# An encoder layer on one core: a row of two one-column float32 products at two places, in place of single ones at three

## The chip, the core and the metric

The kernel runs on one core of a Trainium2 chip. The metric is device time in microseconds (us) of one execution; lower is better. The engines that the text names are TensorE (PE, with its weight loads shown apart as PEld), VectorE (DVE), ScalarE (ACT) and SyncE (SP), whose queue issues most of the transfers.

## What is computed

One layer of a bidirectional encoder, for 256 positions of 2048 channels in float32. What matters here are the four large products:

```python
def reference(x, ...):
    h = rmsnorm(x, norm_mix[i])
    p = h @ w_in[i]                                # 2048 -> 4352 columns
    ...                                            # three token mixers give y_a, y_b, y_c
    x = x + jnp.concatenate([y_a, y_b, y_c], axis=-1) @ w_out[i]      # 2048 -> 2048
    h = rmsnorm(x, norm_ffn[i])
    up = dwconv3(h @ ffn_w_up[i], ffn_conv_w[i], ffn_conv_b[i])       # 2048 -> 11264
    gate, val = jnp.split(up, 2, axis=-1)
    x = x + (jax.nn.silu(gate) * val) @ ffn_w_down[i]                 # 5632 -> 2048
    return rmsnorm(x, norm_final)
```

## The kernel before

Activations lie with channels on the 128 partitions and the 256 positions along the free axis. Every large product is made to float32 accuracy from two parts: a weight tile is loaded as float32 (`raw`), ScalarE rounds it to a part `hi` in the type fp32r (line 115), VectorE subtracts to get the rest `lo` (line 116), and the activations are kept in the same two parts side by side. For each block of 128x128 weights TensorE then does two products into one PSUM bank. This **pair** is the unit of all that follows:

```python
            nc.tensor.matmul(ps, hi[:, s], act[:, k, :, :], start=k == 0, stop=False)
            nc.tensor.matmul(ps[:, :L], lo[:, s], act[:, k, 0, :], start=False, stop=k == nk - 1)
```

The first, line 151, streams 512 columns (both parts of the activations), the second, line 152, streams 256. One output tile of 128 channels takes 16 pairs where the input has 2048 channels (input projection, output projection, up-projection), and 44 pairs in the down-projection. The order on TensorE is program order: 16 tiles of the output projection (`yT` is the input), whose first two tiles are interleaved in two halves of 8 pairs each; 88 tiles of the up-projection (`actB`); 12 tiles of the down-projection (`gT`); and then the last 512 output channels in another form (lines 771 to 783).

Between pairs stand a few small float32 products. `sum_cols` (line 176) does two one-column products in a row for a norm's sum of squares, once after the first up-tile; `rms_rows` (line 194) does one product of 256 columns, after the second up-tile; `gate_head` (line 584) does two products of 128 columns in a row, in the input projection. A float32 product shows in the trace as two records. Three more, `settle()` at line 133, are one-column products of a constant tile of ones; nothing reads what they give. One stands after the first 8 pairs of the output projection, one after its first 32 pairs (two tiles), and one after the third up-tile. The scheduler is told to keep them in program order.

Of the kernel before, what the change touches and what calls it, by code (L numbers as in the profile page):

```python
# [54 lines left out]
def encoder_layer(ctx, tc, a):  # L55
    nc = tc.nc
# [11 lines left out]
    def aux():  # L68
        return psa.tile([P, 512], F32, tag="aux", name="aux")
# [20 lines left out]
    ones = const.tile([P, P], F32, name="ones")  # L90
# [39 lines left out]


    def settle():
        tc.keep_in_program_order(nc.tensor.matmul(aux()[:, 0:1], ones, ones[:, 0:1], start=True, stop=True))

    def split(hi, lo, src):
        nc.scalar.copy(hi, src)
# [36 lines left out]
    def sum_cols(acc):  # L173
        pc = aux()
        for h in range(2):
            nc.tensor.matmul(pc[:, h:h + 1], acc[:, h * P:(h + 1) * P], ones[:, 0:1], start=True, stop=True)
        return pc
# [477 lines left out]
    for c in range(2):  # L655
        for m in range(2):
            chunk_products(head[m], w_out(m), yT, c, KT)
            if c == m == 0:
                settle()
    settle()  # L660
    for m in range(KT):
        ps, sb = (head[m], second_half(head[m])) if m < 2 else proj_tile(w_out(m), yT, KT)
        x = xT[:, m, :]
# [23 lines left out]
    for j in range(NFF):  # L687
        o = []
        for part in range(2):
            m = 2 * j + part  # L690
            ps, sb = up[m] if j == 0 else up_tile(m)
            if m == 2:
                settle()
            nc.vector.tensor_add(sb, ps[:, :L], sb)
            s = tmp("ev")
            nc.vector.tensor_mul(s, sb, rbc2)
            o.append(conv3(s, C_FW + m, C_FW + 88 + m, C_FW + 176 + m, C_FB + m, f"o{part + 1}"))
        sg = tmp("gu")
        nc.scalar.activation(sg, o[0], AF.Silu)
        nc.vector.tensor_mul(sg, sg, o[1])  # L700
        split(gT[:, j, 0, :], gT[:, j, 1, :], sg)
# [54 lines left out]
    for h in range(2):  # L756
        acc.append(psm.tile([P, 512], F32, tag="mm", name="mm"))
        for i in range(NL // P):
            nc.tensor.matmul(acc[h][:, i * P:(i + 1) * P], xT[:, MD + i, h * P:(h + 1) * P], ident, start=i == 0,
                             stop=False)  # L760
# [24 lines left out]
    for c in range(NC):  # L785
# [5 lines left out]
        if c == NKEEP:  # L791
            pc = sum_cols(acc3)
# [143 lines left out]
```

## Time and profile before

| | |
|---|---|
| median of 3 runs | 1071.64 us (1071.21 to 1071.91) |
| the profiled execution | 1071.91 us, of it 1070.0 us from the first to the last instruction |
| TensorE busy | 1059.6 us (99%) |
| VectorE, ScalarE busy | 788.9 us (74%), 578.6 us (54%) |
| weight loads (PEld) busy | 923.6 us (86%) |
| moved by DMA | 202.83 MB, 190 GB/s in the mean |
| mean granted TensorE clock | 0.998 |

Busy time of TensorE is modelled and records of neighbouring products overlap, so that 99% does not say at what pace it works. The pace is read from the distance between the starts of two products of the same kind, for instance from one product of line 151 to the next. The trace's times are printed to 0.01 us.

### The profile page before, as it was taken

Reading aid. Unit: us, or ns where it says so; the run is one execution under the profiler, and the core shown is the slowest. Engines: PE = TensorE matmul, PEld = TensorE weight load, DVE = VectorE, ACT = ScalarE, POOL = GpSimd, SP = SyncE. Lnnn points to the kernel's source line nnn. Section 1 sums busy time; section 2 is a strip of 40 time slices with the busy share of each in tenths; the row PEclk is TensorE's granted clock in tenths of the full one; section 3 lists DMA queues with packets and bytes.
Section 4 is the critical chain, followed back from the end, with each engine's and each line's share of the span. In section 5 each row is a group of like instructions: output and inputs, shape, how many; then the busy total and the mean of one; then the engine's idle time right before and its main releaser. Section 6 shows DMA issues by size and latency. Waiting matters only on the chain.

```text
span 1070.0 us, 15760 instructions
## 1 busy us (share of the span) xinstructions
PE 1059.6 (99%) x5974; PEld 923.6 (86%) x5974; DVE 788.9 (74%) x1241; ACT 578.6 (54%) x876; POOL 1.3 (0%) x14
## 2 busy tenths in 40 slices
PE   9999999999999999999999999999999999999997
PEld 9888898888888888888888888888888888888885
DVE  7899998987768778787777777787876454565344
ACT  7766555555556555555555555555555444454332
POOL 0000000000000000000000000000000000000000
PEclk9999999999999999999999999999999999999999
DMA  8776555655666555655566555655565655666452
GB/s 290 244 229 210 161 164 171 232 172 185 196 194 182 186 186 188 182 192 181 193 181 192 181 192 182 190 184 185 189 188 178 190 183 182 225 214 199 142 191 78
DMA packets 61875, 202.83 MB, mean 190 GB/s; under 512 B 6919, under 2 KB 11752, under 8 KB 61672
## 3 DMA queue, kind: packets, MB, share of 16 engines
q1 hardware_dynamic: 61512, 201.45, 59.2%
q8 instruction: 46, 0.75, 0.3%
q10 hardware_dynamic: 288, 0.39, 0.1%
q14 instruction: 29, 0.24, 0.1%
HBM read 199.72 MB, written 2.10 MB: 189 GB/s over the span
## 4 chain that ended last, share of the span: by engine, by line
PE 96%; DVE 1%; DMA 1%; ACT 1%; issue 0%; SPq 0%; DVEq 0%; ACTq 0%
PE mm L151 57%; PE mm L152 29%; PE mm L781 2%; PE mm L783 2%; PE mm L782 2%; PE mm L264 1%; PE mm L263 1%; PE mm L265 1%; DVE lo L116 1%; DMA head<-in_w_v 1%; PE aux L141 0%; PE aux L142 0%; DMA raw<-in_w_in 0%; PE aux L489 0%; PE aux L140 0%
## 5 line engine op out<-in xcount | busy, mean ns | idle before, releaser
L115 ACT CAST hi<-raw 128x1024 fp32r<-128x1024 f32 (+1 forms) x362 | 373.4, 1031 | 443.7 <-PE mm L151 222.8
L116 DVE TENSOR_TENSOR lo<-raw,hi 128x1024 fp32r<-128x1024 f32 (+1 forms) x362 | 434.6, 1201 | 239.6 <-ACT hi L115 239.0
L151 PE MATMUL mm<-actB,hi 128*128 128x512 f32 x1408 | 497.9, 399 | 0.0
L152 PE MATMUL mm<-actB,lo 128*128 128x256 f32 x1408 | 395.3, 281 | 0.0
L151 PEld LDWEIGHTS mm<-actB,hi 128*128 128x128 f32 x1408 | 264.5, 188 | 66.0 <-DVE actB L668 0.3
L152 PEld LDWEIGHTS mm<-actB,lo 128*128 128x128 f32 x1408 | 265.9, 189 | 0.0
L151 PE MATMUL mm<-gT,hi 128*128 128x512 f32 x528 | 186.6, 399 | 0.0
L152 PE MATMUL mm<-gT,lo 128*128 128x256 f32 x528 | 148.3, 281 | 0.0
L151 PE MATMUL mm<-actA,hi 128*128 128x512 f32 x416 | 148.0, 398 | 0.0
L151 PEld LDWEIGHTS mm<-gT,hi 128*128 128x128 f32 x528 | 99.2, 188 | 24.8
L152 PE MATMUL mm<-actA,lo 128*128 128x256 f32 x416 | 116.2, 279 | 0.0
L152 PEld LDWEIGHTS mm<-gT,lo 128*128 128x128 f32 x528 | 99.7, 189 | 0.0
L151 PEld LDWEIGHTS mm<-actA,hi 128*128 128x128 f32 x416 | 78.1, 188 | 16.9
L151 PE MATMUL mm<-yT,hi 128*128 128x512 f32 x256 | 89.3, 395 | 0.0
L152 PEld LDWEIGHTS mm<-actA,lo 128*128 128x128 f32 x416 | 78.5, 189 | 0.1
L152 PE MATMUL mm<-yT,lo 128*128 128x256 f32 x256 | 71.0, 278 | 0.0
L408 ACT ACTIVATE o<-ev,par 128x256 f32<-128x256 f32 x106 | 63.4, 598 | 7.2 <-DVE ev L403 5.7
L151 PEld LDWEIGHTS mm<-yT,hi 128*128 128x128 f32 x256 | 48.0, 188 | 11.1
L410 DVE SCALAR_TENSOR_TENSOR o<-ev,par,o 128x255 f32<-128x255 f32 x106 | 51.2, 483 | 3.3
L159 ACT COPY sb<-mm 128x256 f32<-128x256 f32 x142 | 51.8, 365 | 0.0
L409 DVE SCALAR_TENSOR_TENSOR o<-ev,par,o 128x255 f32<-128x255 f32 x106 | 50.7, 478 | 0.4 <-ACT o L408 0.4
L152 PEld LDWEIGHTS mm<-yT,lo 128*128 128x128 f32 x256 | 48.1, 188 | 0.0
(226 smaller groups left out, 819.2 us busy)
## 6 DMA issues: line engine op xcount, KB each, us to landing
raw<-in_w_up SPq DMA_DIRECT2D x176, 512.0 KB, 3.5
raw<-in_w_down SPq DMA_DIRECT2D x60, 512.0 KB, 3.6
raw<-in_w_in SPq DMA_DIRECT2D x56, 512.0 KB, 3.6
raw<-in_w_out SPq DMA_DIRECT2D x32, 512.0 KB, 3.5
raw<-in_w_last SPq DMA_DIRECT2D x22, 512.0 KB, 3.5
raw<-in_w_v SPq DMA_DIRECT2D x8, 384.0 KB, 4.4
raw<-in_w_down SPq DMA_DIRECT2D x12, 256.0 KB, 2.6
head<-in_w_v SPq DMA_DIRECT2D x7, 384.0 KB, 6.2
```

Source lines behind the costliest of these rows:

```text
L115: nc.scalar.copy(hi[:, s], raw[:, s])
L116: nc.vector.tensor_sub(lo[:, s], raw[:, s], hi[:, s].bitcast(F32))
L151: nc.tensor.matmul(ps, hi[:, s], act[:, k, :, :], start=k == 0, stop=False)
L152: nc.tensor.matmul(ps[:, :L], lo[:, s], act[:, k, 0, :], start=False, stop=k == nk - 1)
L159: nc.scalar.copy(sb, ps[:, L:])
L263: nc.tensor.matmul(o, actA[:, k, 0, t], hi[:, s], start=k == 0, stop=False)
L408: nc.scalar.activation(o, s, AF.Identity, bias=col(b), scale=col(w1))
L409: nc.vector.scalar_tensor_tensor(o[:, 1:], s[:, :L - 1], col(w0), o[:, 1:], op0=ALU.mult, op1=ALU.add)
L410: nc.vector.scalar_tensor_tensor(o[:, :L - 1], s[:, 1:], col(w2), o[:, :L - 1], op0=ALU.mult, op1=ALU.add)
L781: nc.tensor.matmul(acc[h], lh, hi[:, s], start=False, stop=False)
L782: nc.tensor.matmul(acc[h], lh, lo[:, s], start=False, stop=False)
L783: nc.tensor.matmul(acc[h], ll, hi[:, s], start=False, stop=False)
```

## The change

`settle()` now issues two one-column products in a row, into two columns of one PSUM tile, where it issued one. The call after the two first output tiles is gone. So there are two places with two products each, where there were three places with one.

```diff
     def settle():
-        tc.keep_in_program_order(nc.tensor.matmul(aux()[:, 0:1], ones, ones[:, 0:1], start=True, stop=True))
+        pc = aux()
+        for h in range(2):
+            tc.keep_in_program_order(nc.tensor.matmul(pc[:, h:h + 1], ones, ones[:, 0:1], start=True, stop=True))
...
             chunk_products(head[m], w_out(m), yT, c, KT)
             if c == m == 0:
                 settle()
-    settle()
     for m in range(KT):
         ps, sb = (head[m], second_half(head[m])) if m < 2 else proj_tile(w_out(m), yT, KT)
```

On TensorE, at the first place in the output projection, between the first half of tile `mm_2523` and that of `mm_2524`, the order before was:

```order
L152 MATMUL mm_2523<-yT_519,lo_2527 128x256
L151 MATMUL mm_2523<-yT_519,hi_2526 128x512
L152 MATMUL mm_2523<-yT_519,lo_2527 128x256
L133 MATMUL aux_2547<-ones_85 128x1
L151 MATMUL mm_2524<-yT_519,hi_2550 128x512
L152 MATMUL mm_2524<-yT_519,lo_2551 128x256
```

and in the changed kernel, where lines from 133 on have moved down by one or two numbers, it is:

```order
L154 MATMUL mm_2523<-yT_519,lo_2527 128x256
L153 MATMUL mm_2523<-yT_519,hi_2526 128x512
L154 MATMUL mm_2523<-yT_519,lo_2527 128x256
L135 MATMUL aux_2547<-ones_85 128x1 x2
L153 MATMUL mm_2524<-yT_519,hi_2551 128x512
L154 MATMUL mm_2524<-yT_519,lo_2552 128x256
```

One product has become two at the same spot. Also on TensorE, after the third tile of the up-projection (`mm_3529` before, `mm_3528` in the changed kernel), the order before was:

```order
L152 MATMUL mm_3529<-actB_2521,lo_3554 128x256
L151 MATMUL mm_3529<-actB_2521,hi_3553 128x512
L152 MATMUL mm_3529<-actB_2521,lo_3554 128x256
L133 MATMUL aux_3576<-ones_85 128x1
L151 MATMUL mm_3585<-actB_2521,hi_3587 128x512
L152 MATMUL mm_3585<-actB_2521,lo_3588 128x256
```

and it is now:

```order
L154 MATMUL mm_3528<-actB_2521,lo_3553 128x256
L153 MATMUL mm_3528<-actB_2521,hi_3552 128x512
L154 MATMUL mm_3528<-actB_2521,lo_3553 128x256
L135 MATMUL aux_3575<-ones_85 128x1 x2
L153 MATMUL mm_3585<-actB_2521,hi_3587 128x512
L154 MATMUL mm_3585<-actB_2521,lo_3588 128x256
```

Here too only the second product is added. After the first two output tiles, where the second of the three single products stood, pairs now follow on pairs. The orders of VectorE, ScalarE, GpSimd and SyncE are the same as before.

## Rows read from the trace of the kernel before

**Rows 1.** The page: the span, TensorE's share, the chain that ended last.

```profile
span 1070.0 us, 15760 instructions
PE 1059.6 (99%) x5974; PEld 923.6 (86%) x5974; DVE 788.9 (74%) x1241; ACT 578.6 (54%) x876; POOL 1.3 (0%) x14
...
PE 96%; DVE 1%; DMA 1%; ACT 1%; issue 0%; SPq 0%; DVEq 0%; ACTq 0%
```

**Rows 2.** Line 151 after the third settle: count; durations; first and last start.

```profile
L151 PE MATMUL mm<-actB,hi x1360: 395/398/476, 331.6 to 811.8; 128*128 128x512 f32 x195
L151 PE MATMUL mm<-gT,hi x528: 395/398/403, 812.2 to 998.4; 128*128 128x512 f32 x176
```

**Rows 3.** Line 151 between the second settle and the first wait in the up-projection.

```profile
L151 PE MATMUL mm<-yT,hi x224: 392/395/475, 235.9 to 313.3; 128*128 128x512 f32 x112
L151 PE MATMUL mm<-actB,hi x16: 392/394/395, 313.7 to 318.9; 128*128 128x512 f32 x16
```

**Rows 4.** Engines by stretch: length, busy us (records) by engine, granted clock, DMA share, GB/s.

```profile
236.30:319.10 82.80, 82.80 (x479) 72.38 (x478) 59.05 (x91) 46.61 (x77) 0.00 (x0) 1.00 0.64 194
331.90:998.50 666.60, 666.60 (x3775) 578.11 (x3774) 479.86 (x711) 358.23 (x539) 0.00 (x0) 1.00 0.60 189
```

**Rows 5.** TensorE in order of time (start us, us): third settle, and last pair.

```profile
331.32 0.28 PE L152 MATMUL mm<-actB,lo 128*128 128x256 f32 x1
331.44 0.28 PE L133 MATMUL aux<-ones 128*128 128x1 f32 x2
331.58 0.48 PE L151 MATMUL mm<-actB,hi 128*128 128x512 f32 x1
331.89 0.28 PE L152 MATMUL mm<-actB,lo 128*128 128x256 f32 x1
...
332.71 0.40 PE L151 MATMUL mm<-actB,hi 128*128 128x512 f32 x1
...
333.07 0.40 PE L151 MATMUL mm<-actB,hi 128*128 128x512 f32 x1
...
998.39 0.40 PE L151 MATMUL mm<-gT,hi 128*128 128x512 f32 x1
```

**Rows 6.** TensorE in order of time at the first settle.

```profile
227.10 0.28 PE L133 MATMUL aux<-ones 128*128 128x1 f32 x2
...
227.67 0.40 PE L151 MATMUL mm<-yT,hi 128*128 128x512 f32 x1
...
228.03 0.40 PE L151 MATMUL mm<-yT,hi 128*128 128x512 f32 x1
```

**Rows 7.** TensorE in order of time, from 0.9 us after the second settle.

```profile
236.73 0.39 PE L151 MATMUL mm<-yT,hi 128*128 128x512 f32 x1
...
237.07 0.40 PE L151 MATMUL mm<-yT,hi 128*128 128x512 f32 x1
```

**Rows 8.** TensorE at the two float32 products of the fifth `gate_head`.

```profile
197.87 0.28 PE L152 MATMUL mm<-actA,lo 128*128 128x256 f32 x1
197.99 0.60 PE L584 MATMUL aux<-wsT,vtok 128*128 128x128 f32 x4
198.35 0.48 PE L151 MATMUL mm<-actA,hi 128*128 128x512 f32 x1
```

**Rows 9.** Line 151 in the tile after those products, and in the tile after it.

```profile
L151 PE MATMUL mm<-actA,hi x16: 391/391/476, 198.3 to 203.6; 128*128 128x512 f32 x16
...
L151 PE MATMUL mm<-actA,hi x16: 393/398/478, 204.3 to 209.7; 128*128 128x512 f32 x16
```

**Rows 10.** TensorE around `sum_cols`, after the first up-tile.

```profile
318.89 0.40 PE L151 MATMUL mm<-actB,hi 128*128 128x512 f32 x1
...
319.35 0.50 PE L151 MATMUL mm<-actB,hi 128*128 128x512 f32 x1
...
319.81 0.50 PE L176 MATMUL aux<-ones,acc 128*128 128x1 f32 x4
320.17 0.48 PE L151 MATMUL mm<-actB,hi 128*128 128x512 f32 x1
```

## The prediction

> **What bounds the kernel.** The page comes first: TensorE is busy in 99% of the span, the chain that ended last is TensorE in 96%, and nothing waits long [rows 1]. So time can only come from what TensorE does, and the few float32 products that change are too short to matter by themselves. The question is whether the pairs of lines 151 and 152 always take the same time. The view by line, cut into stretches, says no. The granted clock is 1.00, that is 2.4 GHz, in both of the stretches that I compare, and the pairs are of the same shapes in both [rows 4], yet their pace differs:
>
> - After the second settle the pairs start at 236.73, 237.07, ..., 318.89 [rows 7, 10]. By the count these are 237 steps (240 starts of line 151, of which 236.73 is the third) [rows 3]: 82.16 us / 237 = 0.3467 us a pair. The steps alternate between 0.34 and 0.35.
> - After the third settle they start at 332.71, 333.07, ..., 998.39 [rows 5]. From 333.07, the fifth of 1360 + 528 = 1888 starts [rows 2], it is 665.32 us / 1883 = 0.3533 us a pair. One step in three is 0.36.
>
> I call these the fast and the slow pace. Each is kept without a break until something else comes between two pairs: the slow one lasts from 331.58 to 998.39 through 1888 pairs, over a change of the input from `actB` to `gT`, so it is not the operands' place that sets it. VectorE is busy 480 of 667 us there, 72%, as in the fast stretch (59.1 of 82.8, 71%), and the DMA share is lower (0.60 against 0.64) [rows 4]: no supplier holds the slow stretch back. The pace is a state of TensorE, and what stands between the pairs switches it.
>
> **What switches it.** I read TensorE in order of time at each interruption.
>
> - First settle, one product: slow before, and slow behind it (a step of 0.36 at 227.67) [rows 6].
> - Second settle, one product: the pace turns fast [rows 7].
> - Third settle, one product: fast before, slow behind it [rows 5]. This one costs the kernel most.
> - `sum_cols`, two one-column products in a row at 319.81: fast before and fast up to the third settle, but a wait stands before it: the pair before it starts at 319.35, 0.46 after 318.89 in place of 0.35 [rows 10].
> - The fifth `gate_head`, two products of 128 columns in a row, entered from the alternating fast pace: behind it the products of line 151 take 391 ns in the median, which is fast (the fast stretch has 395, the slow one 398 [rows 2, 3]). The sixth, again two in a row, is entered from there and leaves 398, slow [rows 9].
>
> So a single product does not mean slow and a double one does not mean fast: what counts is at which moment of the rhythm the pairs take up again. That moment can be compared. The up-projection's settle is entered from the fast pace, as the fifth `gate_head` was. There the next pair started 0.48 us after the last product of line 152 (197.87 to 198.35) [rows 8]. At the third settle it started after 331.58 - 331.32 = 0.26. One more product adds its own price. That is, from one product of line 152 to the next, 331.89 - 331.32 = 0.57 where a pair takes 0.35, thus 0.22. Then 0.26 + 0.22 = 0.48: with two products the pairs take up again at the very moment that led to the fast pace behind the fifth `gate_head`. This is why I expect the fast pace for the rest of the up-projection and the whole down-projection. The shown starts are good to 0.01 us, and the paces differ by 0.007, so this match is good evidence and no proof.
>
> **The sum**, against the profiled execution's 1071.91 us, which is 0.27 above the median:
>
> 1. Up- and down-projection from the settle on: 1888 pairs x (0.3533 - 0.3467) = -12.6 us. If they stay slow: 0.
> 2. Output projection. The state at the first settle is untouched by the change, slow; what two products make of it, no row shows. A single one left it slow, the later single one from another moment of the same rhythm made it fast. The bounds are: it turns fast at once, and the 24 pairs up to the old second settle gain 24 x 0.0066 = -0.2; or it stays slow until `sum_cols`, and 240 pairs lose 240 x 0.0066 = +1.6. Three of the six interruptions that I read above end slow; the nearest row is the single product at this same place, entered at this same moment, and it ended slow [rows 6], so I take +1.6.
> 3. The products themselves: three become four, +0.22.
> 4. The second and third up-tile, 32 pairs: 0 if `sum_cols` and `rms_rows` leave them fast as now, +0.2 if not. I take 0.
> 5. The other engines have cover: at the fast pace a tile takes 16 x 0.3467 = 5.55 us, and VectorE's work for one is 480 / 118 = 4.1 us (1888 pairs are 118 tiles of 16). The DMAs would go from 189 to some 193 GB/s, where the fast stretch had 194 [rows 4]. So 0.
>
> Sum: 1071.91 - 12.6 + 1.6 + 0.2 = 1061.1; for the median 0.27 less, **1060.8 us**.
>
> **A rule that speaks against it.** The Trainium skill, page "TensorE: Matmul & The Clock Gate", section "Back-to-back issue gap", gives the distance of two products from their columns and the clock alone, with a small fixed part. Worked out from it (an estimate), a pair of 512 and 256 columns takes 325 ns at 2.4 GHz, whatever stood before it. The trace shows 347 and 353 for the same columns at the same clock [rows 4, 5, 7], so it does not agree that columns and clock are all; by that rule the change would be worth its one added product.
>
> **The rivals.**
>
> - *A: the up-projection stays slow, the output projection turns fast.* For it: two products in a row left a slow pace once, behind the sixth `gate_head` [rows 9]. If the state that reaches the third settle is another than now, because the output projection arrives at `sum_cols` at another moment, the match of 0.48 is void. Time: 1071.64 - 0.2 + 0.2 = 1071.6, no change. Against it: `rms_rows` and 16 pairs lie between. Chance 0.10.
> - *B: pace does not depend on what stands between the pairs.* Then the paces belong to the places in the program, and only the added product counts: 1071.64 + 0.22 = 1071.9. It is the rule above as a mechanism. Against it: the second and third settle change the pace where nothing else does [rows 5, 7]. Chance 0.05.
> - *C: slow everywhere behind the first settle.* This ends on the other side. The fast stretch that the old second settle gave is lost (+1.6), the up-projection's second and third tiles turn slow with it (+0.2), and nothing comes back: 1071.64 + 1.6 + 0.2 + 0.2 = 1073.6. It decides if both doubles lead into the slow pace. For it: the first settle is entered slow, and the state at the third may change with it. Chance 0.21.
> - *D: fast everywhere*: 1060.8 - 1.6 - 0.2 = 1059.0. Chance 0.20.
>
> **How the numbers follow.** Forecast (up and down fast, output projection slow) 0.44, D 0.20, A 0.10, B 0.05, C 0.21. The predicted time is the forecast's, with its own range of 1060.4 to 1061.4 from item 4 and the rounding of the paces (0.0003 x 1888 is 0.6). To leave no more than 2 in 10 out, the whole range must reach from D to C: 1058.7 to 1073.8. A change within 0.2% (2.1 us) is about what cannot be told from none. Faster is forecast and D, 0.64; C lies at +2.0, on that border, so I give slower 0.10; A, B and the other half of C make 0.26 for no change.
>
> **What would show it.** Behind the two products in the up-projection, line 151 should step evenly by 0.35, with no 0.36, up to the last of its 1888 pairs, which should start near 998.4 - 10.8 = 987.6 us. The stretch from the first settle to the up-projection should take 0.3533 a pair if item 2 is right and 0.3467 if D is. A product pair of line 135 should put off the next pair by 0.45. The last stretch (71 us from 999 on, another form of products) should be as long as now. I would be wrong if the steps of 0.36 go on behind the up-projection's two products: then the match of 0.48 has failed, by the state that comes in or by less than the 0.01 us that I can see.

## The result and the profile after

The changed kernel takes 1059.63 us in the median of 4 runs (1059.07 to 1060.96), the kernel before 1071.46 (1071.21 to 1071.91). The ratio is 0.9891 with a 95% interval of 0.9874 to 0.9908: faster by 1.1%. The profiled execution took 1059.53 us with a span of 1057.7, 12.3 us shorter than the span in [rows 1]. Of the cases named ahead it is D: the output projection turned fast too. The time lies 0.6 us above D's 1059.0 and 0.8 below the forecast's own 1060.4 to 1061.4.

The page of the changed kernel, in the same three lines as [rows 1]:

```profile
span 1057.7 us, 15764 instructions
PE 1047.2 (99%) x5976; PEld 917.7 (87%) x5976; DVE 788.4 (75%) x1241; ACT 578.9 (55%) x876; POOL 1.3 (0%) x14
...
PE 96%; ACT 1%; DMA 1%; DVE 1%; issue 0%; DVEq 0%; SPq 0%; ACTq 0%
```

TensorE is as busy as before, 99%, and the chain is TensorE's in 96%. Nothing on the page but the length says that it works faster. The view of one line does; line 151 of before is line 153 now (count; least, median and longest duration in ns; first and last start). First the output projection and the first up-tile, from the first settle to the wait, then the up- and the down-projection behind the second settle:

```profile
L153 PE MATMUL mm<-yT,hi x248: 392/395/473, 227.8 to 313.5; 128*128 128x512 f32 x124
L153 PE MATMUL mm<-actB,hi x16: 392/394/395, 313.8 to 319.0; 128*128 128x512 f32 x16
...
L153 PE MATMUL mm<-actB,hi x1360: 392/395/478, 331.9 to 803.2; 128*128 128x512 f32 x195
L153 PE MATMUL mm<-gT,hi x528: 392/394/395, 803.5 to 986.2; 128*128 128x512 f32 x176
```

The 1888 pairs now start from 331.9 to 986.2, 654.3 us, where they took 666.8 [rows 2], and the median duration is 395 or 394 as in the fast stretch of before [rows 3], not 398. The windows of the same stretches (columns as in [rows 4]) show the granted clock at 1.00, that is 2.4 GHz, as before:

```profile
227.50:319.80 92.30, 92.30 (x534) 80.51 (x533) 66.01 (x103) 51.22 (x83) 0.00 (x0) 1.00 0.60 191
332.00:986.30 654.30, 654.30 (x3776) 572.22 (x3776) 479.73 (x710) 358.79 (x539) 0.00 (x0) 1.00 0.61 193
```

VectorE and ScalarE do the same work in less time (479.73 us of 654.30, before 479.86 of 666.60), and the DMAs move 193 GB/s in place of 189.

In order of time, the changed kernel's first settle:

```profile
227.07 0.40 PE L153 MATMUL mm<-yT,hi 128*128 128x512 f32 x1
227.30 0.28 PE L154 MATMUL mm<-yT,lo 128*128 128x256 f32 x1
227.42 0.50 PE L135 MATMUL aux<-ones 128*128 128x1 f32 x4
227.78 0.47 PE L153 MATMUL mm<-yT,hi 128*128 128x512 f32 x1
...
228.56 0.39 PE L153 MATMUL mm<-yT,hi 128*128 128x512 f32 x1
...
228.91 0.40 PE L153 MATMUL mm<-yT,hi 128*128 128x512 f32 x1
```

and its second one, with the last pair of the down-projection:

```profile
331.46 0.28 PE L154 MATMUL mm<-actB,lo 128*128 128x256 f32 x1
331.58 0.50 PE L135 MATMUL aux<-ones 128*128 128x1 f32 x4
331.94 0.48 PE L153 MATMUL mm<-actB,hi 128*128 128x512 f32 x1
332.26 0.28 PE L154 MATMUL mm<-actB,lo 128*128 128x256 f32 x1
...
332.73 0.39 PE L153 MATMUL mm<-actB,hi 128*128 128x512 f32 x1
...
333.07 0.40 PE L153 MATMUL mm<-actB,hi 128*128 128x512 f32 x1
...
986.19 0.40 PE L153 MATMUL mm<-gT,hi 128*128 128x512 f32 x1
```

The pairs take up 0.48 us after the last product of line 154 at both places, and then step by 0.34 and 0.35 in turn (332.73 to 333.07 is 0.34), with no step of 0.36. The 12.3 us of the span come out of these rows, with the difference of the paces taken from the unrounded quotients, 0.00666 us: 1888 pairs x 0.00666 = -12.6; 24 pairs of the output projection x 0.00666 = -0.16; one product more, +0.22. The rest, some 0.2, is what the other parts differ by: the first settle comes 0.32 us later in this execution (227.42, before 227.10 [rows 6]), and behind the last pair's start 71.5 us are left in place of 71.6.

### The profile page after: what moved, and what is told of

It reads as the page before. It is cut to its first block, busy times and chain, and to the rows that moved or that the text cites. A ratio compares the mean times of both kernels' runs of the same rounds, so it can differ in the third digit from the quotient of the medians.

```text
span 1057.7 us, 15764 instructions
## 1 busy us (share of the span) xinstructions
PE 1047.2 (99%) x5976; PEld 917.7 (87%) x5976; DVE 788.4 (75%) x1241; ACT 578.9 (55%) x876; POOL 1.3 (0%) x14
## 4 chain that ended last, share of the span: by engine, by line
PE 96%; ACT 1%; DMA 1%; DVE 1%; issue 0%; DVEq 0%; SPq 0%; ACTq 0%
PE mm L153 57%; PE mm L154 28%; PE mm L782 2%; PE mm L784 2%; PE mm L783 2%; PE mm L266 1%; PE mm L265 1%; PE mm L267 1%; DMA raw<-in_w_in 1%; ACT hi L115 0%; PE aux L143 0%; PE aux L491 0%; DMA xg<-in_first 0%; PE aux L144 0%; PE aux L142 0%; PE aux L586 0%
## 5 line engine op out<-in xcount | busy, mean ns | idle before, releaser
L153 PE MATMUL mm<-actB,hi 128*128 128x512 f32 x1408 | 488.8, 394 | 0.0
L154 PE MATMUL mm<-actB,lo 128*128 128x256 f32 x1408 | 390.0, 277 | 0.0
L153 PE MATMUL mm<-gT,hi 128*128 128x512 f32 x528 | 183.1, 394 | 0.0
```

## The experiments

**The theories.** *M (moment)*: the pace is a state; a float32 product between two pairs switches it by the moment of the rhythm at which the pairs take up again, and it is kept to the next such product. After the result it got one more step, a guess from numbers of the rows: two fast pairs take 0.6933 us and three slow ones 1.0600, which are 104 and 159 times 0.00667 us. One product puts the pairs off by 0.22 us [rows 5]; within that rounding I chose 0.2233, which is 33.5 times 0.00667. If the moment counts only within 0.00667 us, an odd number of products acts as one, an even number as two. *N or R (number)*: a row of two or more leaves TensorE fast, a single product does not. *Q, S, T*: fast needs the products in the up-projection, or comes in from the output projection, or needs settles somewhere. The first eight runs were one execution each beside one of the kernel before (1072.68 us beside the two singles, the rows of three and four and the double row in the up-projection alone, 1071.61 beside the other four); the up-projection's pace is also read from each trace.

**Without the third single product.** The kernel of before, less one call, whose two lines stand alike in both kernels:

```diff
-            if m == 2:
-                settle()
```

> The kernel of before without the third single product (the one in the up-projection); the two in the output projection stay. Theory M (the pace of the pairs is a state that a float32 product between two pairs switches, by the moment at which the pairs take up again; it keeps until the next such product): the third product was what turned the pace slow, so without it the fast pace behind rms_rows stays, 1888 pairs at 0.3467 us in place of 0.3533: 1071.5 - 12.6 - 0.2 = 1058.7 us, and no step of 0.36 in the up- and down-projection. Rival Q (it needs the two products to be fast there; without them it falls slow by itself, by the load of the other engines): about 1071.3 us.

1058.62 us. M holds, Q falls: without the single product the fast pace behind `rms_rows` simply stays, through 1376 + 528 = 1904 pairs. The third settle of before did nothing but turn it slow.

```profile
L153 PE MATMUL mm<-actB,hi x1376: 392/395/577, 325.4 to 802.2; 128*128 128x512 f32 x197
L153 PE MATMUL mm<-gT,hi x528: 392/394/395, 802.6 to 985.3; 128*128 128x512 f32 x176
```

**Three in a row, and four.** The changed kernel with a number given to `settle()` at both calls, three here and four in the other run (lines between are left out):

```diff
-    def settle():
+    def settle(n=1):
         pc = aux()
-        for h in range(2):
+        for h in range(n):
...
-                settle()
+                settle(3)
...
-                settle()
+                settle(3)
```

> The changed kernel with three one-column products in a row at both places in place of two. Theory M with one more step: the rhythms repeat after multiples of 0.00667 us (0.6933 us for two fast pairs is 104 of them, 1.0600 us for three slow pairs is 159), and one product puts the pairs off by 0.2233 us, 33.5 of them, so that an odd number in a row takes up at the moment of a single one and an even number at that of two. Three should then act as one did: slow behind both places, 1071.5 + 1.6 (output projection) + 0.2 + 0.7 (three more products than before) = 1073.6 us, or 1071.9 us if the output projection is fast and only the up-projection slow. Rival R (a row of two or more always leaves TensorE fast, one product does not): the time of the changed kernel plus two products, 1059.6 + 0.45 = 1060.1 us.

> The changed kernel with four one-column products in a row at both places. Theory M with the half step per product: four act as two, fast behind both places: 1059.6 + 4 x 0.22 = 1060.5 us. Rival R says the same. If the number matters in another way than odd and even (a theory in which each count lands elsewhere), it may be slow: 1073.9 us.

Three: 1074.56 us. Four: 1061.47 us. Both lie 1.0 us above what was expected; the kernel before took 1072.68 beside them, 1.2 above its median. Rival R falls with the three. Line 153 of the kernel with three, behind the first and behind the second row:

```profile
L153 PE MATMUL mm<-yT,hi x248: 395/398/478, 228.1 to 315.5; 128*128 128x512 f32 x124
...
L153 PE MATMUL mm<-actB,hi x1360: 395/398/476, 334.2 to 814.5; 128*128 128x512 f32 x195
L153 PE MATMUL mm<-gT,hi x528: 395/398/403, 814.8 to 1001.0; 128*128 128x512 f32 x176
```

The median is 398 at both places, the slow pace, as behind one product; with four it is 395 at both. In between, `sum_cols` had turned the slow pace of the output projection fast here, so that the up-projection's three products were entered from the fast pace as always.

**Two in a row in the up-projection alone, and in the output projection alone.** The other products stay single. The first, against the changed kernel (lines between are left out):

```diff
             if c == m == 0:
-                settle()
+                settle(1)
+    settle(1)
...
             if m == 2:
-                settle()
+                settle(2)
```

The second has `settle(2)` at the first place, `settle(1)` at the last, and none between.

> The kernel of before with its two single products in the output projection, and two in a row in place of the third in the up-projection. Theory M: the up-projection's products are entered from the same moment as before, so two turn the rest fast: 1071.5 - 12.6 + 0.2 = 1059.1 us; the first 24 pairs of the output projection are slow and the others fast, as before. Rival S (the gain came in from the output projection, by another state at the up-projection's products): slow, 1071.7 us.

> Two products in a row in the output projection (as in the changed kernel), and the single one of before in the up-projection. Theory M: the output projection is fast from the first settle on (-0.2 us for 24 pairs), the single product in the up-projection is entered from the same moment as before and turns it slow: 0.2 us under the kernel before, 1071.3 us where that takes 1071.5. Rival S (the state that the output projection is in carries over to the up-projection): 12.6 us less, 1058.9.

The first took 1060.40 us (1072.68 for before beside it), the second 1072.34 (1071.61 beside it). Line 153 behind the up-projection's row, in the first and in the second:

```profile
L153 PE MATMUL mm<-actB,hi x1360: 392/395/477, 332.8 to 804.0; 128*128 128x512 f32 x195
```

```profile
L153 PE MATMUL mm<-actB,hi x1360: 395/398/476, 331.9 to 812.2; 128*128 128x512 f32 x195
```

So the gain is made at the up-projection's products alone, S falls, and what the output projection does is worth no more than the scatter of single executions.

**No settle at all.**

> No one-column products at line 133 at all. Theory M: the output projection keeps the slow pace in which it begins, 264 pairs, until the wait and the two products of sum_cols; what rms_rows leaves behind is fast, since it was in all rows seen so far, and nothing disturbs it: by the kernel of before, -12.6 us (up, down), +1.6 us (240 pairs of the output projection and the first up-tile), -0.7 us (three products): 1059.8 us where before takes 1071.5. Rival T (fast needs settle products somewhere): up and down slow, 1072.4 us.

1060.18 us. T falls. The trace shows both parts of what M expected: the output projection is slow (first two lines), and behind `rms_rows` the pairs are fast (last two), with the even rhythm of the fifth `gate_head`'s row, 391 ns. That rhythm is as fast as the alternating one: the 527 steps from 804.1 to 986.8 are 0.3467 us each.

```profile
L153 PE MATMUL mm<-yT,hi x247: 395/398/403, 227.5 to 314.4; 128*128 128x512 f32 x124
L153 PE MATMUL mm<-actB,hi x13: 395/398/403, 314.7 to 319.0; 128*128 128x512 f32 x13
...
L153 PE MATMUL mm<-actB,hi x1376: 391/391/580, 326.9 to 803.8; 128*128 128x512 f32 x197
L153 PE MATMUL mm<-gT,hi x528: 391/391/391, 804.1 to 986.8; 128*128 128x512 f32 x176
```

**The same products one pair later.** This is the sharpest test of moment against number: nothing is added or taken away, the up-projection's row only moves behind the first pair of the fourth up-tile. In the code, a count of the pairs made calls `settle`, and the other calls are taken out (lines between are left out; the double row has `{456: 2, 753: 2}`).

```diff
+    done = [0]
+    SETTLE = {456: 1, 480: 1, 753: 1}
...
             nc.tensor.matmul(ps[:, :L], lo[:, s], act[:, k, 0, :], start=False, stop=k == nk - 1)
+            done[0] += 1
+            if done[0] in SETTLE:
+                settle(SETTLE[done[0]])
```

> The kernel of before, with the third single product one pair later: behind the first pair of the fourth up-tile in place of ahead of it. Theory M: in the fast rhythm two neighbouring pairs are half a period of 0.00667 us apart (0.3433 us is 51.5 of them), so one pair later does what one product more does, and the single product should now leave the fast pace: 12.6 us less than before, 1058.9 us where before takes 1071.5. Rival N (the number of products in the row decides, one leaves slow): the time of before.

> The changed kernel, with the two products of the up-projection one pair later, behind the first pair of the fourth up-tile. Theory M: by the same half period the double row should now turn the up- and down-projection slow: 12.6 us more than the changed kernel, 1072.2 us. Rival N (two in a row leave fast): 1059.6 us.

The single product one pair later: 1058.58 us, fast. The double row one pair later: 1071.73, slow. Both changed sides, and N falls. Line 156 (the first product of a pair in these two files) behind the row, the single one first:

```profile
L156 PE MATMUL mm<-actB,hi x1359: 391/394/476, 331.3 to 802.2; 128*128 128x512 f32 x195
L156 PE MATMUL mm<-gT,hi x528: 392/394/396, 802.5 to 985.2; 128*128 128x512 f32 x176
```

```profile
L156 PE MATMUL mm<-actB,hi x1359: 395/398/481, 331.9 to 811.8; 128*128 128x512 f32 x195
L156 PE MATMUL mm<-gT,hi x528: 395/398/403, 812.2 to 998.4; 128*128 128x512 f32 x176
```

And the double row in order of time, in the slow one of the two:

```profile
331.44 0.28 PE L157 MATMUL mm<-actB,lo 128*128 128x256 f32 x1
331.55 0.50 PE L135 MATMUL aux<-ones 128*128 128x1 f32 x4
331.91 0.48 PE L156 MATMUL mm<-actB,hi 128*128 128x512 f32 x1
...
332.69 0.40 PE L156 MATMUL mm<-actB,hi 128*128 128x512 f32 x1
...
333.06 0.40 PE L156 MATMUL mm<-actB,hi 128*128 128x512 f32 x1
```

Here the pairs take up 0.47 us after the last product (331.44 to 331.91), and at the fast settle of the changed kernel 0.48: at 0.01 us the rows of a fast and of a slow case can hardly be told apart.

**One single product in all, and the double row of the output projection alone.** The single product stands behind 10 pairs of the output projection, and in one more run behind 9. All but that run have four executions each, with the first experiment once more among them; the kernel before took 1071.98 us beside them:

> One single product in the whole kernel, two pairs later than the first settle of before (behind 10 pairs of the output projection), nothing in the up-projection. Theory M: the slow rhythm has three moments; two pairs behind that of the first settle is the moment of the second settle of before (the step of 0.36 just done), which turned fast. So fast from there to the end, with two products less than before: 1071.5 - 12.6 - 0.45 - 0.15 = 1058.3 us. Rival N (one product does not turn the output projection fast here): 1059.9 us.

> The same with the single product one pair later than the first settle of before (behind 9 pairs). It is the third of the three moments of the slow rhythm, for which no run has a row with this product. Theory M lets it be either; by the offset worked out from the starts at the first and the second settle I expect it to stay slow until sum_cols: 1059.9 us. If it turns fast: 1058.3 us.

> The changed kernel without its two products in the up-projection. Theory M: they were not needed, since rms_rows leaves the pace fast; the time is that of the changed kernel less two products, 1059.6 - 0.45 = 1059.2 us, 0.988 of before. Rival Q (fast needs them there): 1071.7 us.

> The kernel with the two single products of before in the output projection and none in the up-projection, once more and timed. Theory M: 1058.9 us, 0.988 of before; beside the kernel with one single product it should be 0.4 us longer, which five rounds may just tell.

| kernel | us, median | ratio to before (95%) |
|---|---|---|
| one single product behind 10 pairs | 1058.37 (1057.67 to 1058.51) | 0.9868 (0.9852 to 0.9885) |
| one single product behind 9 pairs (one execution) | 1060.56 | |
| two in a row behind 8 pairs, none later | 1058.94 (1058.15 to 1060.65) | 0.9877 (0.9862 to 0.9893) |
| single ones behind 8 and 32 pairs, none later | 1059.17 (1058.79 to 1059.35) | 0.9877 (0.9862 to 0.9892) |

Each pace came as expected: behind 10 pairs the single product leaves the output projection fast (median 395), behind 9 pairs slow (398). These two also answer a rival that the row moved by one pair leaves open, that a product inside a tile acts otherwise than one between two tiles. Both stand inside a tile, entered from the same slow pace, and one ended fast and the other slow; of the single products of before, all between tiles, two ended slow and one fast [rows 5, 6, 7]. By their medians all three with four executions are as fast as the changed kernel or a little faster. The order of the medians is what the number of products and of slow pairs gives, but the intervals overlap, so that no one of them is shown to be the fastest.

## Why the prediction was right, and the step that was not

The term that carries the time was right, the choice for the output projection was not. The time lies inside the whole range because that was drawn wide enough to take in D and C; the forecast's own range missed it by 0.8 us.

- *The pace is a state that float32 products switch*: right. It is shown by the two kernels in which the same products stand one pair later, and by one to four products in a row.
- *Item 1, -12.6 us*: right in size. From the first to the last start the 1888 pairs took 12.5 us less than in [rows 2]. That they would turn fast rested on the match of 0.48, on which more below.
- *Item 2, the output projection stays slow, +1.6*: wrong. It turned fast at once, worth -0.16. The step that failed was to take the single product at the same place [rows 6] as the nearest row. By theory M one product more moves the moment by half a period, so a single product that leaves slow was no evidence for two. The runs show it from that one moment in order: none slow, one slow, two fast, three slow, four fast.
- *Item 3*: three products became four, and the price stands: from one product of line 154 to the next over the double row of the up-projection it is 332.26 - 331.46 = 0.80 us, less a pair of 0.35 and so 0.45 for two.
- *Item 4*: 0, as taken. `sum_cols` left the changed kernel fast, and `rms_rows` left the fast pace in all 14 traces, also where `sum_cols` had left a slow one (no settle at all). So the second and third up-tile cost nothing, and wherever the up-projection has products of its own they meet the same alternating rhythm.
- *Item 5, the cover*: right, no wait came up at the faster pace.
- *The match of 0.48*: it gave the right pace by luck, for 0.47 to 0.48 us is what a row of two takes here whatever pace follows. Behind the sixth `gate_head` of the kernel before the pairs also took up 0.48 us after the last product (203.87 to 204.35), and went on slow [rows 9]:

```profile
203.87 0.28 PE L152 MATMUL mm<-actA,lo 128*128 128x256 f32 x1
203.98 0.61 PE L584 MATMUL aux<-wsT,vtok 128*128 128x128 f32 x4
204.35 0.48 PE L151 MATMUL mm<-actA,hi 128*128 128x512 f32 x1
```

So the distance from the last product does not tell the moment in the rhythm, and the trace of before already showed it. What is left of the evidence is one row: the fifth `gate_head`, entered from the alternating pace as the up-projection's products are, ended fast. It did not lead to the same state either: behind it the rhythm was the even one (391 ns), behind the changed kernel's up-settle it is the alternating one (395).

- *The rule of the Trainium skill* (page "TensorE: Matmul & The Clock Gate", section "Back-to-back issue gap"): the section gives the formula behind the 325 ns as the gap of an isolated product, and says that in a stream with a weight load for each product both together set the spacing. The pairs here are such a stream (5976 weight loads for 5976 products on the page of the changed kernel), so the prediction asked more of the formula than the section does. Rival B, that the pace does not depend on what stands between the pairs, falls by the runs: the granted clock is 1.00 from 335 to 980 us in all 14 traces, and the pace there is slow in four of them and fast in ten.

What stays open is what in TensorE makes the two paces. That the moment counts within a period of 0.00667 us is not shown: the figure comes from the paces and from a price of a product that the rows give only as 0.22 us. The runs with odd and even numbers and with one pair more came out as it says, but none measures it by itself.

## What to carry to other kernels

Where TensorE is the bound and looks busy all the time, read the distance between the starts of equal products in each stretch, not the busy share: the slow pace was 2% longer here, at the same 99% busy. In this kernel a tiny product between long rows of pairs set the pace of the hundreds of us that follow, so that adding, dropping or moving one by a single pair is worth a try. A measured gain from such a product says nothing about another place or another count. Before tuning such a product, try the kernel without it: here the last one was only harmful.

## What was not expected of the hardware

The pace of a stretch is not a property of its code. The program up to the tile behind the fifth `gate_head` is the same in both kernels; in [rows 9] that tile ran at 391 ns, and in the changed kernel's trace at 398:

```profile
L153 PE MATMUL mm<-actA,hi x16: 393/398/478, 198.7 to 204.0; 128*128 128x512 f32 x16
```

Two traces of one and the same file, the kernel with two single products and its repetition, both have 398 there, so the runs do not tell whether the execution or something in the built program makes the difference.

The first 8 pairs of the output projection, however, were slow in all 14 traces, though the tile behind the sixth `gate_head` was slow in some (398 in [rows 9]) and fast in others (395 in the changed kernel). The pairs behind `rms_rows` were fast in all, though in the kernel without settles the second up-tile, ahead of it, was slow (398). These two places thus led to one pace from either, while the settles carry the moment on.
